# Pinning ScalarE's copy of the memory probabilities, and what follows it, in a hybrid decoder step

## The chip, the cores and the metric

The kernel runs on one core of one Trainium2 chip. The metric is device time in microseconds (us). Engines are named as the profile names them: PE is TensorE (PEld its weight loads), DVE is VectorE, ACT is ScalarE, POOL is GpSimd and SP is SyncE, which here issues most DMAs.

## The reference

One inference step of a single decoder layer, for a prompt of 4096 tokens and for 64 sample tokens (8 sequences of 8), width 1024:

```python
h = _rmsnorm(x, g_pre)
z = h @ w_in
cb, cc, ch, cg, q, k, v, ag, mq, mg = _split_cols(z)
u = cc * ch
conv = conv_w[0] * up[:, 0:t] + conv_w[1] * up[:, 1:t + 1] + conv_w[2] * up[:, 2:t + 2]
out_a = jax.nn.silu(cg) * cb * conv
out_b = jax.nn.silu(ag) * o_b      # sliding-window attention, window 128, with sinks
out_c = jax.nn.silu(mg) * o_c      # cross-attention into 256 memory tokens
y = jnp.concatenate([out_a, out_b, out_c], axis=-1) @ w_out
return x + _rmsnorm(y, g_post), new_conv, new_k, new_v
```

Window attention has 8 query heads and 2 key heads of 64; memory attention has 4 heads of 64. The sample tokens attend to cached keys and values instead of the prompt's.

## The kernel before

For more than the first half of the span the kernel projects the input (`x @ w_in`) and leaves queries, keys, values and gates in device memory. The last part, which the change touches, does attention and the output projection together, interleaved on PE.

**Attention** goes in chunks of 256 tokens (`Chunk`, 16 of them) and in halves of 128 tokens, numbered h = 2 x chunk + half. Each half has three pieces of code that are called between matmuls of the output projection. `first_half(h)` first turns the memory probabilities of the half before (`memory_transposes`, L1360 on: eight transposes on PE into the tile `tx`, then one ScalarE copy to `xp`, L1367), then issues the window scores of this half (`window_scores`, L1331), then the products of probabilities and values of the half before (`products`, L1380 on, matmuls L1388, L1394 and L1059), and then the window probabilities (ScalarE copies L1340, Vector masked copies L1341, maxima, exponentials L1287, shares L1295). `memory_half(h)` has the memory scores (L1353), their maxima, exponentials (L1178) and GpSimd's scaling (L1190). `second_half(h)` turns the window probabilities (`window_turns`, L1376), copies them on ScalarE (L1305) and masks them twice on GpSimd (L1310, L1313).

PSUM is held by three pools: `w` with two tiles of two banks, `x` with one tile of two banks, and `z` with two tiles of one bank. `tx` and the products' banks are both the one `x` tile, and so are the memory scores.

**The output projection** takes two blocks of 128 tokens (`Block`). Chunks 0 to 2 are done as plain blocks of 16 steps. Chunks 3 to 15 are done as pairs (`Pair.run`, L1721 on) with seven products in place of eight for part of the matrix, 30 steps each; a step is three matmuls (L1737), since operands are split into a rounded part and a rest (`lows`: a ScalarE cast, L1676, and a Vector subtraction, L1679). The products of a pair accumulate in four quarters of the result: c12 (block 0, right half), c21 (block 1, left), c11 (block 0, left) and c22 (block 1, right), which share the two `z` tiles in turn. Each quarter is copied or added out of its bank (`done`, L1744; `added`, L1753), squared on ScalarE for the norm (L1740), multiplied by the gain (L1749 or L1756), and at last the factor is computed (L1652 on Vector, L1653 on GpSimd) and the residual added and stored (`finish`, L1658 and L1661). The last pair's c22 is done in two pieces of 256 columns, with the whole sample between (`sample`, L1981 on), and the 64 sample tokens' own block (`Block(32)`) ends there.

Inside a pair, with its first step at e, `first_half` of the odd half is called at step e + 12, of the even half at e + 24; `memory_half` at + 16 and + 27; `second_half` at + 18 and + 32, which is step 2 of the next pair. `plain_parts` of the next pair is called at e + 20, `row_sums` at e + 27, `window_parts` at e + 4 and e + 7, `diagonal_sum` at e + 9 and `column_differences` at e + 11.

**Order.** PE's order is that of the program up to pair 12, and again from step 18 of pair 15 (`tc.manual_schedule`). All else is ordered by a planner, which takes instructions by their place in the program when their operands are there by its own model of time. `tc.keep_in_program_order(x)` adds one edge: x is issued behind the instruction of its engine that the program named just before it. It orders; it does not wait, and it keeps nothing else from standing in between. The engines other than PE work their queues in the order so made, waits included.

The sample's attention is cut into stages (generators `sample_mem(0)`, `sample_mem(1)`, `sample_window()`), and the table `steps` says at which (pair, step) each next stage is called. The scratch tiles `s3`, `s4` and `sum` have one buffer each.

## Time and profile before

| What | Value |
|---|---|
| Runs, median of 3 (lowest, highest) | 1544.68 us (1540.74, 1551.7) |
| Profiled execution, whole | 1541.58 us |
| Its span | 1539.9 us |
| PE busy | 1502.5 us, 98% |
| PEld busy | 1383.1 us, 90% |
| DVE busy | 1203.5 us, 78% |
| ACT busy | 842.8 us, 55% |
| POOL busy | 395.3 us, 26% |

The busy times are of the profiled execution, whose span is the time between its first and last instruction. A line L1367 is a line of the kernel before. In rows of a timeline the first number is the start in us from the span's beginning and the second the duration; instructions of one line are merged, and the bracket gives the idle time of the engine before the row and what released it. The ends of matmuls are modelled by the profiler. A tile's buffer numbers are left out.

### The profile page before, as it was taken

Reading aid. Unit: us, or ns where it says so; the run is one execution under the profiler, and the core shown is the slowest. Engines: PE = TensorE matmul, PEld = TensorE weight load, DVE = VectorE, ACT = ScalarE, POOL = GpSimd, SP = SyncE. Lnnn points to the kernel's source line nnn. Section 1 sums busy time; section 2 is a strip of 40 time slices with the busy share of each in tenths; the row PEclk is TensorE's granted clock in tenths of the full one; section 3 lists DMA queues with packets and bytes.
Section 4 is the critical chain, followed back from the end, with each engine's and each line's share of the span. In section 5 each row is a group of like instructions: output and inputs, shape, how many; then the busy total and the mean of one; then the engine's idle time right before and its main releaser. Section 6 shows DMA issues by size and latency. Waiting matters only on the chain. (4 is left out here: it accounts for less than half of the span.)

```text
span 1539.9 us, 30911 instructions
## 1 busy us (share of the span) xinstructions
PE 1502.5 (98%) x11497; PEld 1383.1 (90%) x11497; DVE 1203.5 (78%) x2088; ACT 842.8 (55%) x2066; POOL 395.3 (26%) x576
## 2 busy tenths in 40 slices
PE   9999999999999999999999999999999999999997
PEld 9999999999999999999999998878777777777775
DVE  6779878899888777996777688777777777777864
ACT  6776566575222222454445456666666666666652
POOL 0223322221300000000201302344444444444531
PEclk9999999999999999999999999999999999999999
DMA  9989999877755333777876978998555555555543
GB/s 262 206 209 260 262 271 270 283 245 272 193 180 180 126 126 126 255 248 272 244 252 201 252 267 248 285 260 192 166 164 165 162 160 156 155 159 156 155 149 109
DMA packets 217241, 319.70 MB, mean 208 GB/s; under 512 B 37381, under 2 KB 143365, under 8 KB 217061
## 3 DMA queue, kind: packets, MB, share of 16 engines
q1 hardware_dynamic: 196757, 273.54, 59.7%
q0 software_dynamic: 19616, 43.15, 10.2%
q8 instruction: 91, 1.49, 0.4%
q10 hardware_dynamic: 720, 1.05, 0.2%
q14 instruction: 57, 0.47, 0.1%
HBM read 208.50 MB, written 110.15 MB: 207 GB/s over the span
## 5 line engine op out<-in xcount | busy, mean ns | idle before, releaser
L375 DVE TENSOR_TENSOR z<-c,z 128x520 f32<-128x520 f32 (+1 forms) x308 | 195.0, 646 | 85.3 <-PE c L368 84.0
L1737 PE MATMUL y_c<-wo,pw 128*128 128x512 f32 (+1 forms) x636 | 159.2, 391 | 1.3 <-DVE pw L1679 0.7
L1737 PEld LDWEIGHTS y_c<-wo,pw 128*128 128x128 f32 x636 | 114.6, 188 | 27.4 <-issue 2.2
L1287 ACT ACTIVATE sm<-sm,wnm 128x128 f32<-128x128 f32 x256 | 99.4, 389 | 70.5 <-DVE wnm L1281 70.5
L1190 POOL TENSOR_SCALAR xp<-xp,xrd 128x256 f32<-128x256 f32 x128 | 67.3, 545 | 141.7 <-DVE xrd L1184 141.7
L1178 ACT ACTIVATE xp<-xs,xnm 128x256 f32<-128x256 f32 x128 | 58.8, 470 | 23.2 <-DVE xnm L1170 23.2
L1341 DVE COPY_PREDICATED sm<-wmask,ws 128x512 f32<-128x512 uint8 x60 | 40.5, 728 | 36.8 <-ACT sm L1340 36.8
L737 POOL CAST wmask<-negs 128x256 uint8<-128x256 f32 x1 | 1.0, 1049 | 263.4 <-DMA negs<-in_wmask 263.4
L1313 POOL TENSOR_SCALAR_AFFINE_SELECT wpt<-wpt 128x512 f32<-128x512 f32 x64 | 57.3, 915 | 38.5 <-ACT wpt L1305 38.1
L1637 PE MATMUL y<-wo,mh 128*128 128x512 f32 x192 | 64.6, 399 | 0.2 <-ACT y L1646 0.2
L1331 PE MATMUL ws<-kst,q 128*128 128x256 f32 (+1 forms) x480 | 55.7, 297 | 0.0
L276 ACT ACTIVATE nat<-nat 104x1024 f32<-104x1024 f32 x40 | 42.3, 1057 | 20.2 <-DMA nat<-in_x_p 20.2
L407 ACT CAST zh<-z 128x520 fp32r<-128x520 f32 x56 | 33.3, 625 | 34.8 <-DVE z L375 31.9
L377 ACT COPY z<-c 128x520 f32<-128x520 f32 (+1 forms) x44 | 24.3, 553 | 50.7 <-PE c L368 47.5
L1331 PEld LDWEIGHTS ws<-kst,q 128*128 128x128 f32 (+1 forms) x480 | 46.4, 187 | 4.1
L1658 DVE SCALAR_TENSOR_TENSOR xr<-yn,yst,xr 128x1024 f32<-128x1024 f32 (+2 forms) x34 | 46.6, 1376 | 3.0 <-POOL yst L1653 3.0
L1287 ACT ACTIVATION_READ_ACCUMULATOR sm<-sm,wnm 128x1 f32 x256 | 47.8, 187 | 0.0
L1310 POOL TENSOR_SCALAR_AFFINE_SELECT wpv<-wpt 128x512 f32<-128x512 f32 x62 | 45.5, 754 | 8.7 <-ACT wpt L1305 8.6
L1740 ACT ACTIVATE s<-yn 128x512 f32<-128x512 f32 (+1 forms) x53 | 33.4, 631 | 26.0 <-DVE yn L1753 22.4
L1295 DVE TENSOR_TENSOR sm<-sm,wrd 128x512 f32<-128x512 f32 x64 | 45.0, 703 | 1.1
L1637 PEld LDWEIGHTS y<-wo,mh 128*128 128x128 f32 x192 | 36.1, 188 | 8.9 <-issue 1.0
L164 POOL DMA_DIRECT2D md<-th x48 | 26.2, 547 | 68.1 <-DVE th L425 58.6
(1034 smaller groups left out, 5568.1 us busy)
## 6 DMA issues: line engine op xcount, KB each, us to landing
q<-qd SPq DMA_DIRECT2D x168, 128.0 KB
xr<-in_x_p SPq DMA_DIRECT2D x32, 512.0 KB
nat<-in_x_p SPq DMA_DIRECT2D x39, 416.0 KB
o_yp<-xr SPq DMA_DIRECT2D x31, 512.0 KB
kst<-qd SPq DMA_DIRECT2D x112, 128.0 KB
md<-th POOLq DMA_DIRECT2D x48, 260.0 KB
qd<-zh SPq DMA_DIRECT2D x48, 260.0 KB
qd<-z SPq DMA_DIRECT2D x48, 260.0 KB
```

Of the source, the lines that this page charges most:

```text
L276: S.activation(t[:RG], t[:RG], AF.Square, accum_out=r[:RG, i : i + 1])
L375: add = lambda dst, other: V.tensor_tensor(dst, c, other, op=ALU.add)
L1178: S.activation(p[:, i, :], s[:, i, :], AF.Exp, bias=nm[:, i : i + 1], scale=SCALE, accum_out=den[:, i : i + 1])
L1190: G.tensor_scalar(p[:, i, :], p[:, i, :], self.rds[h][:, i : i + 1], 0.5, op0=ALU.mult, op1=ALU.mult)
L1287: S.activation(sm[:, hh, :], sm[:, hh, :], AF.Exp, bias=nm[:, hh : hh + 1], scale=SCALE, accum_out=den[:, hh : hh + 1])
L1295: V.tensor_tensor(sm, sm, rd.unsqueeze(2).to_broadcast([P, 4, P]), op=ALU.mult)
L1310: G.affine_select(pv.rearrange("p (h q) -> p h q", h=4), p3, pattern=[[0, 4], [-1, P]], compare_op=ALU.is_gt, fill=0.0, base=0, channel_mu ...
L1313: G.affine_select(p3, p3, pattern=[[0, 4], [1, P]], compare_op=ALU.is_ge, fill=0.0, base=0, channel_multiplier=-1)
L1331: TE.matmul(out(kvh, col, bank), q(kvh, col, bank)[r], k(kvh, part)[r], start=first, stop=True, skip_group_check=not first, **place)
L1637: TE.matmul(acc, self.hl[l][:, k], wo[k][p][:, r], start=k + i == 0, stop=k + i == KT + 1)
L1658: x = V.scalar_tensor_tensor(self.xr[:m, cs], yn[:m, cs], st[:m, 3:4], self.xr[:m, cs], op0=ALU.mult, op1=ALU.add)
L1737: TE.matmul(acc, a[:, l, k], w[:, r, cs], start=first, stop=k == len(ws) - 1 and i == 2, skip_group_check=not new)
```

## The change

Five things change.

1. In `memory_transposes` the copy L1367 is pinned behind the ScalarE instruction named before it.
2. In a pair, `column_differences` still issues its GpSimd subtraction at its step, but the cast and the rest (`lows`, now pinned) are put in a list `between`, which `first_half` empties behind the window scores and before the products. In the last pair they come at once.
3. The Squares of a pair are pinned. `added` is cut in two: the addition stays, and `scaled` (Square, factor, gain) comes behind it; for the quarter c11 it goes into `between` also, with the block's end.
4. The intermediate of c22 is kept in `s3` until the end of the pair and no longer in `y[1]`, whose right half holds the raw differences; the sample's scratch tile moves from `s3` to `sum`.
5. The steps at which the sample's stages are called are moved, and the sample's residual is added in two halves of the columns between the pieces of the last quarter, where it was added in one, ahead of them in the program. One entry that finished a block at the first step of a pair is now only there for pair 14, at its step 27.

```diff
-            S.copy(self.xp.rearrange("p j a n -> p j (a n)"), tx)
+            tc.keep_in_program_order(S.copy(self.xp.rearrange("p j a n -> p j (a n)"), tx))
...
-                    junk = sums["s3"].tile([P, 512], F32, tag="s3", name=f"junk_s{p}")
+                    junk = sums["sum"].tile([P, 512], F32, tag="sum", name=f"junk_s{p}")
...
-        def finish(self, yn, st, dst, queued, last=False):
-            m = self.m
-            for cs in (slice(0, 512), slice(512, D)) if last else (slice(0, D),):
+        def finish(self, yn, st, dst, queued, last=False, part=None):
+            m, halves = self.m, (slice(0, 512), slice(512, D))
+            for cs in halves if last else (slice(0, D),) if part is None else (halves[part],):
...
-            self.lows(t, raw)
+            return lambda pinned=False: self.lows(t, raw, pinned)
...
-            self.sums_of(self.y[1][:, 512:], t, (self.mix(slice(0, 4), 1), self.mix(slice(0, 4), 0), ALU.subtract))
+            self.differences = self.sums_of(self.y[1][:, 512:], t, (self.mix(slice(0, 4), 1), self.mix(slice(0, 4), 0), ALU.subtract))
...
-                square(n, p, y[n][:, cs], s4)
+                square(n, p, y[n][:, cs], s4, True)
...
-            def added(n, p, acc, s, junk, cs=None):
-                cs = cs or (left_, right_)[p]
-                V.tensor_tensor(y[n][:, cs], acc, s, op=ALU.add)
-                square(n, p, y[n][:, cs], junk)
+            def added(n, p, acc):
+                cs = (left_, right_)[p]
+                V.tensor_tensor(y[n][:, cs], acc, s3 if n else y[n][:, cs], op=ALU.add)
+
+            def scaled(n, p, pinned=False):
+                cs = (left_, right_)[p]
+                square(n, p, y[n][:, cs], s4, pinned)
                 self.blocks[n].factor(st[n])
                 (V if n else G).tensor_tensor(y[n][:, cs], y[n][:, cs], gpost[:, cs], op=ALU.mult)
...
-            V.tensor_tensor(y[1][:, right_], s3, c11, op=ALU.add)
+            V.tensor_tensor(s3, s3, c11, op=ALU.add)
...
-            added(0, 0, c11, y[0][:, left_], s4)
-            ends(0)
+            added(0, 0, c11)
             if not last:
                 c22 = psum("z", f"y{c}_c22")
+                between.append(lambda: (scaled(0, 0, True), ends(0)))
                 product(c22, self.down[0], t["T6"], True)
                 product(c22, self.w[1], plain(1, range(4, 8)), False)
-                added(1, 1, c22, y[1][:, right_], s4)
+                added(1, 1, c22)
+                scaled(1, 1)
                 ends(1)
                 return
+            scaled(0, 0)
+            ends(0)
             finish_block()
-            sample()
+            rest = sample()
...
-                x = V.tensor_tensor(y[1][:, half], c22, y[1][:, half], op=ALU.add)
+                x = V.tensor_tensor(y[1][:, half], c22, s3[:, cs], op=ALU.add)
                 if p:
-                    tc.keep_in_program_order(x)
+                    rest(True, 0)
...
+            rest(True, 1)
             ends(1)
...
             chunks[c].window_scores(i)
+        while between:
+            between.pop(0)()
         banks = before[0].products(before[1]) if before else None
...
-        at(e, lambda: left.pop(0)(True) if len(left) > 1 else None)
+        if c == NCH - 2:
+            at(e + 27, lambda: left.pop(0)(True))
...
+        at(e + (9 if c == NCH - 1 else 11), lambda p=p: p.differences(True) if p.c == NCH - 1 else between.append(lambda: p.differences(True)))
...
-    steps = (((14, 16), (15, 3), (15, 6), (15, 8), (15, 10)), ((15, 8), (15, 14), (15, 16), (15, 18), (15, 21)),
-             ((14, 13), (14, 24), (15, 4), (15, 8)))
-    at(start_of(NCH - 2) + 27, lambda: left.pop(0)(True))
+    steps = (((14, 16), (14, 28), (15, 4), (15, 6), (15, 8)), ((15, 8), (15, 13), (15, 15), (15, 17), (15, 20)),
+             ((14, 13), (15, 6), (15, 15), (15, 18)))
...
-            finish_block(True)
+            return left.pop()
```

More of the change, by code (lines that the diff above doesn't have):

```diff
@@ L1647, in run @@
             self.factor(st)
-            left.append(lambda queued: self.finish(yn, st, dst, queued))
+            left.append(lambda queued, part=None: self.finish(yn, st, dst, queued, part=part))
         def factor(self, st, p=1):
@@ L1699, in row_sums @@
             raw = sums["sum"].tile([P, 512], F32, tag="sum", name=f"sum{self.c}")
-            self.sums_of(raw, t, *((self.mix(slice(2, 4), n), self.mix(slice(0, 2), n), ALU.add) for n in range(2)))
+            self.sums_of(raw, t, *((self.mix(slice(2, 4), n), self.mix(slice(0, 2), n), ALU.add) for n in range(2)))()
         def window_parts(self, n):
@@ L1707, in diagonal_sum @@
             self.diagonal = self.parts("pd")[:, :, 0:2]
-            self.sums_of(sums["sum"].tile([P, 512], F32, tag="sum", name=f"diag{self.c}"), self.diagonal, (self.mix(slice(2, 4), 0), self.mix(slice(0, 2), 1), ALU.add))
+            self.sums_of(sums["sum"].tile([P, 512], F32, tag="sum", name=f"diag{self.c}"), self.diagonal, (self.mix(slice(2, 4), 0), self.mix(slice(0, 2), 1), ALU.add))()
         def column_differences(self):
@@ L1737, in product, with square @@
                         TE.matmul(acc, a[:, l, k], w[:, r, cs], start=first, stop=k == len(ws) - 1 and i == 2, skip_group_check=not new)
-            def square(n, p, src, junk):
-                S.activation(junk, src, AF.Square, scale=float(D) ** -0.5, accum_out=st[n][:, p : p + 1])
+            def square(n, p, src, junk, pinned=False):
+                x = S.activation(junk, src, AF.Square, scale=float(D) ** -0.5, accum_out=st[n][:, p : p + 1])
+                if pinned:
+                    tc.keep_in_program_order(x)
             def done(n, p, acc):
@@ L1915, in hybrid_layer @@
     what, pending = {}, []
+    between = []
     def at(n, fn):
```

## The prediction

> **What bounds the kernel now.** I read the page first, then the waits of TensorE (PE), then busy time pair by pair, then the timeline of one pair on the four engines, and last the end of the span.
>
> ```profile
> span 1539.9 us, 30911 instructions
> ```
>
> The profiled execution took 1541.58 us, so 1.7 us lie around this span. The waits of PE (total us, times, longest) over the whole span have one large entry:
>
> ```profile
> PE wo L1388 <- ACT xp L1367: 19.6, 13, 1.7
> ```
>
> The attention products wait for ScalarE's copy of the turned memory probabilities. Busy time in one pair of the third part (length of the stretch, then PE, PEld, DVE, ACT, POOL):
>
> ```profile
> 1160.90:1198.30 37.40, 35.67 (x240) 29.10 (x239) 29.32 (x66) 23.95 (x82) 17.84 (x24) 1.00 0.58 159
> ```
>
> PE idles 1.73 us of this pair's 37.4 us and no other engine comes near to being full, so this is a TensorE kernel with one hole per pair. The timeline shows the hole in the odd half (start, duration, engine, line; idle before in brackets):
>
> ```profile
> 1159.87 2.90 PE L1737 MATMUL y_c<-wo,pw 128*128 128x512 f32 x12
> 1162.60 1.04 PE L1366 MATMUL xt<-ident,xp 128*128 128x128 f32 x8
> 1163.39 1.86 PE L1331 MATMUL ws<-kst,q 128*128 128x256 f32 x16
> 1166.88 0.43 PE L1388 MATMUL wo<-wpv,vt 64*64 64x256 f32 x2 [1.63 <-ACT xp L1367]
> ```
>
> ```profile
> 1163.97 0.62 ACT L1676 CAST pc<-yn 128x512 fp32r<-128x512 f32 x1 [4.54 <-POOL yn L1693]
> 1164.50 0.58 ACT L1744 COPY yn<-y_c 128x512 f32<-128x512 f32 x1
> 1165.11 0.63 ACT L1740 ACTIVATE s<-yn 128x512 f32<-128x512 f32 x1
> 1165.65 0.19 ACT L1740 ACTIVATION_READ_ACCUMULATOR s<-yn 128x1 f32 x1
> 1165.74 0.99 ACT L1367 COPY xp<-xt 128x1024 f32<-128x1024 f32 x1
> 1166.63 1.07 ACT L1340 COPY sm<-ws 128x512 f32<-128x512 f32 x2
> ```
>
> Transposes and products share the single two-bank tile x, so the products need the copy finished. The transposes end at 1162.60 + 1.04 = 1163.64; the copy starts only at 1165.74, behind the rounding of the differences (which stood idle 4.54 us for GpSimd, and holds ACT's queue meanwhile), the quarter's copy and its Square. The even half has the same order without the hole:
>
> ```profile
> 1179.55 1.03 PE L1366 MATMUL xt<-ident,xp 128*128 128x128 f32 x8
> 1180.34 1.86 PE L1331 MATMUL ws<-kst,q 128*128 128x256 f32 x16
> 1182.30 0.43 PE L1388 MATMUL wo<-wpv,vt 64*64 64x256 f32 x2
> ```
>
> ```profile
> 1180.53 0.63 ACT L1740 ACTIVATE s<-yn 128x512 f32<-128x512 f32 x1 [1.67 <-DVE yn L1753]
> 1181.07 0.19 ACT L1740 ACTIVATION_READ_ACCUMULATOR s<-yn 128x1 f32 x1
> 1181.16 0.99 ACT L1367 COPY xp<-xt 128x1024 f32<-128x1024 f32 x1
> 1182.06 1.07 ACT L1340 COPY sm<-ws 128x512 f32<-128x512 f32 x2
> ```
>
> The scores end at 1182.20, the products start at 1182.30: 0.1 lost.
>
> **The copy, odd half.** It is now pinned behind the last ScalarE instruction traced before it, the quarter's copy L1744. That needs only the c12 group, which ends at 1159.87 + 2.90 = 1162.77, so with its 0.58 it is over at 1163.4. The pinned copy then starts when the transposes end, about 1163.68, and ends at 1164.67, 0.58 us ahead of the end of the scores (1163.39 + 1.86 = 1165.25). The whole 1.63 goes.
>
> Not all 13 waits are of this kind. Two others:
>
> ```profile
> 1034.68 0.43 PE L1388 MATMUL wo<-wpv,vt 64*64 64x256 f32 x2 [1.66 <-ACT xp L1367]
> ```
>
> ```profile
> 1055.98 0.43 PE L1388 MATMUL wo<-wpv,vt 64*64 64x256 f32 x2 [0.25 <-ACT xp L1367]
> ```
>
> The first is half 8, at step 89, the second step of the right half of plain block 5. What was traced before it on ScalarE is the Square of that block's left half (L1646), which the change does not move, so the pin puts the copy behind just that: 1.66 stays. The second is pair 3 and goes. Left are 11 waits in pairs 4 to 14, 17.7 us. Gain: 19.6 - 1.66 = 17.9 us.
>
> **What is late next in the odd half.** The rounding starts one copy later (0.89, from 1165.74 to 1166.63): 1164.57; the window scores' copies start 0.53 after that, 1165.10, which is 0.15 ahead of the products where it was 0.25 ahead. On Vector, the low part of the differences now stands ahead of the masked copy:
>
> ```profile
> 1165.87 0.69 DVE L1749 TENSOR_TENSOR yn<-yn,gpost 128x512 f32<-128x512 f32 x1 [0.55 <-ACT s L1740]
> 1167.25 1.35 DVE L1341 COPY_PREDICATED sm<-wmask,ws 128x512 f32<-128x512 uint8 x2 [0.69 <-ACT sm L1340]
> ```
>
> The masked copy began 0.37 after the products; with the rounding over at 1165.19 and a subtraction of about 0.65 behind it (estimated as the gain multiply L1749, same shape) it begins at 1165.85, 0.6 after them. So the window softmax comes 0.2 us later relative to PE. Its last consumer:
>
> ```profile
> 1173.97 0.69 DVE L1295 TENSOR_TENSOR sm<-sm,wrd 128x512 f32<-128x512 f32 x1
> ```
>
> ```profile
> 1174.55 1.03 PE L1376 MATMUL wt<-ident,sm 128*128 128x128 f32 x8
> ```
>
> The second four transposes, at about 1174.95, need this result, there at 1174.66: 0.29 of cover, 0.2 used. Cost 0; if the cover is gone, 0.1 to 0.4 per pair.
>
> **The Squares.** Square (0,1) is traced behind the window exponentials and pinned there; its gain multiply (L1749, 0.69) leaves 1165.87 and lands between the window shares and the maxima of the memory scores, or after them; the planner decides. In the first case the memory exponentials shift by some 0.65 (its 0.69, less a little overlap). They feed GpSimd's chain into the even half's products:
>
> ```profile
> 1177.36 1.84 POOL L1190 TENSOR_SCALAR xp<-xp,xrd 128x256 f32<-128x256 f32 x4 [5.46 <-DVE xrd L1184]
> 1179.16 1.22 POOL L1310 TENSOR_SCALAR_AFFINE_SELECT wpv<-wpt 128x512 f32<-128x512 f32 x2
> 1180.33 1.22 POOL L1313 TENSOR_SCALAR_AFFINE_SELECT wpt<-wpt 128x512 f32<-128x512 f32 x2
> ```
>
> The selects end at 1181.55, with products possible at 1182.20: cover 0.65, eaten by that shift. Besides, Square (1,0) now runs behind the turned windows' copies, so its multiply, also 0.69, falls beside these selects. What that costs GpSimd, the next odd half shows:
>
> ```profile
> 1195.44 1.61 POOL L1310 TENSOR_SCALAR_AFFINE_SELECT wpv<-wpt 128x512 f32<-128x512 f32 x2
> 1197.00 2.65 POOL L1313 TENSOR_SCALAR_AFFINE_SELECT wpt<-wpt 128x512 f32<-128x512 f32 x2
> ```
>
> ```profile
> 1196.48 1.64 DVE L1658 SCALAR_TENSOR_TENSOR xr<-yn,yst,xr 128x1024 f32<-128x1024 f32 x1
> ```
>
> Beside Vector work the same selects took 0.39 and 1.43 us longer a pair. One multiply should cost the 0.39 end. So the even half loses between -0.1 (the present 0.1 goes) and 0.65 + 0.39 - 0.65 = 0.39, or 1.43 if the multiply costs the other end. I take 0.15, halfway between the first two, as it depends on the planner's order: 11 x 0.15 = 1.7 us given back.
>
> The Trainium skill ("GPSIMD Engine Reference", section 1, Specifications) says that GpSimd's SBUF interfaces are shared with VectorE and contended by Vector instructions with two SBUF inputs. The longer selects agree. By that rule, with every such overlap counted, the give-back would be the 0.39 end, 11 x 0.39 = 4.3, and the sum 2.6 us higher.
>
> Even half, rest: the copy is pinned behind the next pair's plain-part casts (traced at step 20, run long before), so it goes from 1180.6 to 1181.6; the Square follows and the scores' copies start 0.1 later. Cost 0. The s3 tile, now read to the pair's end, is a rival below. The sample's scratch tile costs nothing; its instructions are the same.
>
> **The end.** From the sample's steps to PE's last matmul, and the last stores:
>
> ```profile
> 1484.00:1530.30 46.30, 44.14 (x276) 32.78 (x274) 27.37 (x66) 17.49 (x48) 10.22 (x19) 1.00 0.37 131
> ```
>
> ```profile
> 1532.28 1.42 DVE L1658 SCALAR_TENSOR_TENSOR xr<-yn,yst,xr 128x512 f32<-128x512 f32 x2 [0.45 <-POOL yst L1653]
> ```
>
> ```profile
> 1534.91 0.52 SPq L1661 DMA_DIRECT2D o_ys<-xr  x1
> ```
>
> PE idles 2.2 us here. Moving the sample's window scores from step 24 of pair 14 to step 6 of pair 15 (with its load on SP, its small matmuls, and the copies, masks and exponentials behind them), its transposes to step 15 and its values and three stores to step 18 takes Vector work off the new pair's start and puts it beside later products. Bounds: all 2.2 gained, or as much lost; I take 1.0 gained. The stores are queued behind the sample's own load on SP, and ahead of nothing but the final stores some steps later.
>
> At the very end Vector updates block 31's two halves (to 1533.70) and then the sample, whose store goes out last at 1534.91. Now the sample's halves go first, in Vector's gaps before 1532.28, and block 31 ends about 0.1 later, so the last store leaves near 1533.8: 1.1 gained. SP issues one store more.
>
> **Sum.** 17.9 - 1.7 + 1.0 + 1.1 = 18.3 us; 1541.6 - 18.3 = 1523.3. The three runs shown lie from 1540.74 to 1551.7, median 1544.68, so the profiled one is a low one; I say 1523.5.
>
> **Rivals.** (a) GpSimd becomes the even half's last. The planner puts the multiply ahead of the maxima, and the second multiply costs up to 1.4: about 0.9 per pair, halfway between 0.39 and 1.43, 11 x 0.9 = 9.9 instead of 1.7: 1531.5. For: a cover of 0.65 against a shift of as much. Against: Vector's instruction there is short.
>
> (b) The pin does not do what it says. It orders the copy behind one instruction; it keeps nothing else from being put in between, and a late predecessor makes it late, as at 1034.68. Then only the end gains: 1539.5. Against: ScalarE had nothing ready but the rounding, now behind it.
>
> (c) Slower: the s3 tile. It has one buffer. The last quarter's addition (L1753) now reads it, and the next pair's copy of c12 (L1765) has to wait for that, while c12's next matmuls wait for the copy:
>
> ```profile
> 1191.88 0.67 DVE L1753 TENSOR_TENSOR yn<-y_c,yn 128x512 f32<-128x512 f32 x1
> ```
>
> ```profile
> 1192.54 0.60 ACT L1765 COPY s<-y_c 128x512 f32<-128x512 f32 x1
> ```
>
> ```profile
> 1194.10 2.92 PE L1737 MATMUL y_c<-wo,pr 128*128 128x512 f32 x12
> ```
>
> Today the addition ends at 1192.55 just as the copy starts, and the copy ends 0.96 before PE wants the bank. An addition later by more than 0.9 stalls PE in 12 pairs. If it slips by 3.7 us behind the maxima and shares that share Vector with it, PE loses 2.8 x 12 = 34 us, and the time is 1541.6 - 18.3 + 34 = 1557. For: the addition is not pinned and already runs late. Against: nothing that the change moves stands directly ahead of it.
>
> **How the numbers follow.** Forecast 0.58, with its own range 1518 to 1527 (bounds of the even half and the end); (a) 0.25; (b) 0.08; (c) 0.09. About 1%, 15.4 us, is what a measurement of this kernel can tell from no change. Of the forecast 0.54 lies beyond that and 0.04 within; (a) and (b) are within. So faster 0.54, same 0.37, slower 0.09. The range goes from 1517 to 1535, which takes in the forecast and (a).
>
> **What would show it.** In the new waits of PE, L1388 behind ACT L1367 should show about 1.7 us in one or two waits, not 19.6 in 13, and a pair should last about 35.9 us, not 37.4. In the odd half ScalarE should read L1744, L1367, L1676, L1340. Rival (a) would show L1388 or L1366 waiting for POOL L1313 or L1190 eleven times; (b) another ScalarE instruction between L1744 and L1367; (c) PE L1737 on pr waiting for ACT L1765. I am wrong if the pair's length does not shrink, or if the waits go and the pair still has a hole.

## The result, and the profile after

| | Kernel before | Changed kernel |
|---|---|---|
| Median of 12 runs each (lowest, highest) | 1547.09 us (1540.74, 1552.42) | 1530.89 us (1527.32, 1541.16) |
| Profiled execution, whole (its span) | 1541.58 us (1539.9) | 1541.16 us (1539.4) |

The ratio is 0.9902, with a 95% interval of 0.9879 to 0.9925: 1% faster, 15.2 us of 1547.09 (11.6 to 18.7; the two medians differ by 16.2), where 18.3 were forecast. The time itself, forecast at 1523.5, lies 7.4 us higher; 5.5 of that is the base, as the sum was made on an execution of 1541.6 us and the kernel before has a median of 1547.09 over twelve runs.

The two profiled executions are almost equally long, so they can't be compared by their spans: the changed kernel's happens to be the longest of its twelve. Windows show where it was lost. Each row gives the length of a stretch, then busy time of PE, PEld, DVE, ACT and POOL with their numbers of instructions, the granted clock of TensorE, the DMA share and GB/s. The cut is the first turning of memory probabilities. The kernel before:

```profile
0.00:818.34 818.34, 815.36 (x6777) 810.20 (x6778) 665.27 (x930) 410.66 (x694) 121.64 (x188) 1.00 0.75 224
818.34:1539.90 721.56, 687.18 (x4723) 572.93 (x4721) 538.21 (x1159) 432.10 (x1372) 273.67 (x389) 0.99 0.65 189
```

The changed kernel:

```profile
0.00:831.47 831.47, 823.12 (x6777) 816.48 (x6778) 666.19 (x930) 410.19 (x694) 118.79 (x188) 1.00 0.75 221
831.47:1539.40 707.93, 687.67 (x4723) 570.28 (x4721) 541.92 (x1160) 432.95 (x1372) 272.69 (x389) 0.99 0.68 192
```

The input projection, which the change doesn't touch, took 13.1 us more in this one execution; among the profiles of this study it takes 818 to 832 us. From the cut to the end the changed kernel is 13.6 us shorter at the same busy time of PE: what went is idle time. All that follows is read behind the cut.

The waits of PE over the span (total us, times, longest), the changed kernel:

```profile
PE y_c L1737 <- DVE yn L1755: 3.8, 11, 0.6
PE wt L1376 <- DVE sm L1295: 2.1, 11, 0.4
...
PE wo L1388 <- ACT xp L1367: 1.7, 1, 1.7
```

The row that stood at 19.6 us in 13 waits is down to the one at half 8. In its place stand two rows, 5.9 us together, of which the first wasn't there and the second stood at 0.3 us in one wait. One pair, from the transposes of an even half to those of the next (the kernel before measured between odd halves):

```profile
1162.60:1199.57 36.97, 35.24 (x237) 28.75 (x236) 28.89 (x65) 23.95 (x82) 17.41 (x24) 1.00 0.59 161
```

```profile
1155.11:1190.90 35.79, 35.31 (x237) 28.59 (x236) 29.26 (x65) 24.02 (x82) 17.14 (x24) 1.00 0.60 166
```

A pair is 1.18 us shorter, with 0.48 us of idle time left in it, where it had 1.73. The odd half, changed kernel, PE and ScalarE (start, duration, engine, line; idle before in brackets):

```profile
1175.32 1.03 PE L1366 MATMUL xt<-ident,xp 128*128 128x128 f32 x8
1176.11 1.85 PE L1331 MATMUL ws<-kst,q 128*128 128x256 f32 x16
1177.89 0.43 PE L1388 MATMUL wo<-wpv,vt 64*64 64x256 f32 x2
```

```profile
1175.52 0.59 ACT L1746 COPY yn<-y_c 128x512 f32<-128x512 f32 x1 [3.34 <-PE y_c L1737]
1176.44 1.01 ACT L1367 COPY xp<-xt 128x1024 f32<-128x1024 f32 x1 [0.34 <-PE xt L1366]
1177.36 0.62 ACT L1676 CAST pc<-yn 128x512 fp32r<-128x512 f32 x1
1177.88 1.07 ACT L1340 COPY sm<-ws 128x512 f32<-128x512 f32 x2
```

ScalarE's order is the predicted one (L1744 has become L1746): the copy L1367 waits for the transposes and for nothing else, and the products follow the scores without a hole. The window scores' copies now start with the products; they started 0.25 us ahead of them before. Where the two new waits arise, on VectorE and PE:

```profile
1167.62 0.67 DVE L1755 TENSOR_TENSOR yn<-y_c,s 128x512 f32<-128x512 f32 x1
```

```profile
1167.64 0.38 PE L1912 MATMUL vtp<-ident,vT 128*128 128x128 f32 x2
1168.35 1.65 PE L1737 MATMUL y_c<-wtT,pa 128*128 128x512 f32 x6 [0.33 <-DVE yn L1755]
```

```profile
1184.93 0.66 DVE L1169 TENSOR_REDUCE xmx<-xs 128x2 f32<-128x512 f32 x1
1185.51 0.68 DVE L1295 TENSOR_TENSOR sm<-sm,wrd 128x512 f32<-128x512 f32 x1
```

```profile
1185.58 0.60 PE L1376 MATMUL wt<-ident,sm 128*128 128x128 f32 x4
1186.34 0.63 PE L1376 MATMUL wt<-ident,sm 128*128 128x128 f32 x4 [0.16 <-DVE sm L1295]
```

First, the second product of the next pair (T4) needs the bank of the old pair's last quarter, which is free when VectorE has done that quarter's addition (L1755, L1753 before). Second, the last four transposes of the odd half's window probabilities need the second share (L1295), which stands behind a maximum of the memory scores.

### The profile page after: what moved, and what is told of

Its sections match the earlier page's. It is cut to its first block, busy times and chain, and to the rows that moved or that the text cites. A ratio compares the mean times of both kernels' runs of the same rounds, so it can differ in the third digit from the quotient of the medians.

```text
span 1539.4 us, 30947 instructions
## 1 busy us (share of the span) xinstructions
PE 1510.8 (98%) x11497; PEld 1386.8 (90%) x11497; DVE 1208.1 (78%) x2089; ACT 843.1 (55%) x2066; POOL 391.5 (25%) x576
## 4 chain that ended last, share of the span: by engine, by line
PE 68%; DVE 12%; issue 4%; DMA 4%; ACT 3%; POOL 1%; SPq 1%; DVEq 0%; ACTq 0%; POOLq 0%
PE c L368 49%; PE y_c L1737 9%; PE y L1637 2%; DVE sm L1295 2%; DVE sm L1341 1%; PE xt L1366 1%; DVE xr L1658 1%; DMA kst<-qd 1%; PE ws L1331 1%; DVE xmx L1169 1%; ACT sm L1287 1%; DMA nat<-in_x_p 1%; DVE wmx L1279 1%; PE mem_acc L790 1%; DMA zs<-in_w_out 1%
## 5 line engine op out<-in xcount | busy, mean ns | idle before, releaser
L1737 PE MATMUL y_c<-wo,pw 128*128 128x512 f32 (+1 forms) x636 | 158.4, 391 | 0.5 <-DVE yn L1775 0.5
L1737 PEld LDWEIGHTS y_c<-wo,pw 128*128 128x128 f32 x636 | 114.1, 188 | 27.2 <-issue 5.4
L1310 POOL TENSOR_SCALAR_AFFINE_SELECT wpv<-wpt 128x512 f32<-128x512 f32 x62 | 51.8, 848 | 58.5 <-ACT wpt L1305 58.4
L1658 DVE SCALAR_TENSOR_TENSOR xr<-yn,yst,xr 128x1024 f32<-128x1024 f32 (+2 forms) x35 | 52.4, 1501 | 3.1 <-POOL yst L1653 3.0
L1295 DVE TENSOR_TENSOR sm<-sm,wrd 128x512 f32<-128x512 f32 x64 | 44.8, 700 | 1.1
L1367 ACT COPY xp<-xt 128x1024 f32<-128x1024 f32 x30 | 30.4, 1014 | 27.1 <-POOL wpv L1310 16.1
L1737 PE MATMUL y_c<-wtT,pa 128*128 128x512 f32 x156 | 41.1, 400 | 3.8 <-DVE yn L1755 3.8
```

The source lines that it names most:

```text
L1295: V.tensor_tensor(sm, sm, rd.unsqueeze(2).to_broadcast([P, 4, P]), op=ALU.mult)
L1658: x = V.scalar_tensor_tensor(self.xr[:m, cs], yn[:m, cs], st[:m, 3:4], self.xr[:m, cs], op0=ALU.mult, op1=ALU.add)
L1737: TE.matmul(acc, a[:, l, k], w[:, r, cs], start=first, stop=k == len(ws) - 1 and i == 2, skip_group_check=not new)
```

## The experiments

Nine kernels were run, each beside runs of the kernel before on the same chip, which took 1546.93 us there for e1 to e4, 1549.3 for e5 to e7 and 1545.88 for e8 and e9 (medians). So the ratios are what is comparable; the length of a pair, read in each profile, is much sharper than any total. Edits shift the lines: L1737, L1746, L1755 and L1775 of the changed kernel have higher numbers in some rows below, and the text says what they are.

| Kernel | Median us (runs) | Ratio to before, 95% | A pair, us |
|---|---|---|---|
| changed kernel | 1530.89 (12) | 0.990 (0.988 to 0.992) | 35.79 |
| e1, differences only | 1540.2 (7) | 0.995 (0.993 to 0.998) | 36.52 |
| e2, Squares only | 1535.18 (4) | 0.992 (0.989 to 0.994) | 36.52 |
| e3, old end | 1529.14 (4) | 0.987 (0.985 to 0.990) | 35.80 |
| e4, addition first | 1529.9 (4) | 0.988 (0.985 to 0.990) | 35.79 |
| e5, no hole at half 8 | 1529.94 (4) | 0.988 (0.986 to 0.989) | 35.80 |
| e6, quarter chain | 1531.21 (6) | 0.989 (0.987 to 0.991) | 35.90 |
| e7, e6 with e3 and e5 | 1533.85 (5) | 0.990 (0.988 to 0.992) | 35.90 |
| e8, early cast | 1526.39 (6) | 0.987 (0.984 to 0.989) | 35.63 |
| e9, e8 with e5 | 1528.75 (6) | 0.988 (0.985 to 0.991) | 35.63 |

**e1: the Squares go back**, unpinned and right behind the additions; only the rounding of the differences is moved.

```diff
-                square(n, p, y[n][:, cs], s4, True)
+                square(n, p, y[n][:, cs], s4)
...
             added(0, 0, c11)
+            scaled(0, 0)
+            ends(0)
...
-                between.append(lambda: (scaled(0, 0, True), ends(0)))
```

> The changed kernel with the Squares (and what follows them) put back where they were; only the rounding of the differences is moved. ScalarE's order in the odd half is then quarter's copy, Square, xp copy, rounding. Theory (the rounding, which waits for GpSimd, is what held the copy): the copy ends 0.15 us ahead of the scores, the eleven waits of 1.6 us stay away, and a pair lasts 35.6 to 36.0 us (35.8 in the changed kernel, 37.0 before), since TensorE's new wait for the last quarter's addition (L1755, 0.33 a pair) shrinks and the one for the window shares (L1295, 0.16) grows. Rival (the Square also has to go): its 0.63 us stays in front, about 0.5 us of wait per odd half remains, and a pair lasts 36.3 or more.

A pair took 36.52 us, and the hole was in neither place. The waits of PE in e1:

```profile
PE wt L1376 <- DVE sm L1295: 11.5, 13, 1.1
PE y L1632 <- DVE mh_s L1605: 2.1, 1, 2.1
PE wo L1388 <- ACT xp L1367: 1.6, 1, 1.6
```

Its odd half, ScalarE, then VectorE, then PE:

```profile
1164.56 0.63 ACT L1740 ACTIVATE s<-yn 128x512 f32<-128x512 f32 x1
...
1165.19 0.99 ACT L1367 COPY xp<-xt 128x1024 f32<-128x1024 f32 x1
1166.09 0.61 ACT L1676 CAST pc<-yn 128x512 fp32r<-128x512 f32 x1
1166.61 1.07 ACT L1340 COPY sm<-ws 128x512 f32<-128x512 f32 x2
```

```profile
1173.35 0.68 DVE L1169 TENSOR_REDUCE xmx<-xs 128x2 f32<-128x512 f32 x1
...
1174.02 0.68 DVE L1169 TENSOR_REDUCE xmx<-xs 128x2 f32<-128x512 f32 x1
...
1174.82 0.69 DVE L1295 TENSOR_TENSOR sm<-sm,wrd 128x512 f32<-128x512 f32 x1
```

```profile
1175.65 0.63 PE L1376 MATMUL wt<-ident,sm 128*128 128x128 f32 x4 [1.06 <-DVE sm L1295]
```

The Square ahead of the copy makes the scores' copies 0.28 us late against the products, which start at 1166.33 without a wait, and the planner now puts both maxima (2 x 0.68) ahead of the second share. So L1388's wait goes by moving the rounding alone, and what moving the Squares buys is the place where the time would come back. The totals of e1 hold another loss, behind the last pair (the 2.1 us row). The new wait behind L1755 isn't in e1's list: the quarter c11's Square stands in its old place there, and the even half runs as before the change.

**e2: the differences go back**, rounded at their own step, unpinned; only the Squares are moved.

```diff
-        at(e + (9 if c == NCH - 1 else 11), lambda p=p: p.differences(True) if p.c == NCH - 1 else between.append(lambda: p.differences(True)))
+        at(e + (9 if c == NCH - 1 else 11), lambda p=p: p.differences(p.c == NCH - 1))
```

> The changed kernel with the rounding of the differences given at its step again; only the Squares are moved. ScalarE's order in the odd half is rounding, quarter's copy, xp copy. Theory: the rounding still waits for GpSimd, the copy starts 1.45 us late, and L1388 waits 1.0 us for L1367 in each odd half; a pair lasts 36.8 us, and some 11 of the changed kernel's gain are lost. Rival (the Squares were in the way): the waits stay away and a pair lasts 35.8.

The wait of PE in e2:

```profile
PE wo L1388 <- ACT xp L1367: 12.4, 12, 1.7
```

Without half 8 that is 10.7 us in 11 waits: ten of 0.9 us, near the theory's 1.0, and one of 1.64. A pair took 36.52 us (36.8 expected). So with the Square alone out of the way the hole shrinks by 0.7 us; what is left is the rounding, which holds the queue while it waits for GpSimd. With the rounding alone out of the way (e1) the hole closes, but the softmax behind it comes late. For the pair's length both had to leave. The wait behind L1755 is in e2's list, at 3.5 us in 11 waits, so it comes with the moved Squares.

**e3: the old end**, that is the sample's steps and the order of the last stores as before the change.

```diff
-    steps = (((14, 16), (14, 28), (15, 4), (15, 6), (15, 8)), ((15, 8), (15, 13), (15, 15), (15, 17), (15, 20)),
-             ((14, 13), (15, 6), (15, 15), (15, 18)))
+    steps = (((14, 16), (15, 3), (15, 6), (15, 8), (15, 10)), ((15, 8), (15, 14), (15, 16), (15, 18), (15, 21)),
+             ((14, 13), (14, 24), (15, 4), (15, 8)))
...
-            return left.pop()
+            finish_block(True)
```

> The changed kernel with the sample's steps and the sample's last addition as they were before. Theory (the new end is worth nothing, as the two profiles show): pairs last 35.8 us, and from the last even half to the last matmul, and from there to the end, it takes 51.5 and 9.6 us, within 0.5 of the changed kernel's 51.9 and 9.6. Rival (the prediction's terms): 1.0 and 1.1 us longer.

Nothing was lost by it; the stretch came out shorter than the changed kernel's by more than the 0.5 us that the theory allowed. From the last transposes of memory probabilities to PE's last matmul it took 51.12 us (51.86 in the changed kernel, 51.51 before), and from there to the end of the span 9.41 (9.58 and 9.63). The new end cost 0.7 and 0.2 us: six other profiles that have it (e2, e4, e5, e6, e8 and e9) show 51.70 to 51.83 and 9.57 to 9.58, so two profiles of one end differ by less. It is one profile of the old end behind these pairs, and behind those of e6 the old end took longer (e7, below).

**e4: the addition first.** On VectorE the next pair's row-sum subtraction is pinned behind the last quarter's addition instead of standing ahead of it.

```diff
-            self.sums_of(raw, t, *((self.mix(slice(2, 4), n), self.mix(slice(0, 2), n), ALU.add) for n in range(2)))()
...
+            S.copy(t[:, 0], raw)
+            behind.append(lambda: self.low(t, raw))
...
                 added(1, 1, c22)
+                while behind:
+                    behind.pop(0)()
```

> The changed kernel with Vector's subtraction for the next pair's row sums put behind the last quarter's addition, which today waits behind it. Theory (TensorE's new wait of 0.33 us a pair is Vector's queue in front of that addition, which frees the bank): the wait for L1755 goes, nothing else takes its place, and a pair lasts 35.45 us, 12 pairs 4 us less than the changed kernel. Rival (something else is late by as much): the wait moves to the rows' product, behind the subtraction, and a pair stays at 35.8.

The wait went from the list and the pair stayed at 35.79: the rival's length, for neither of the reasons given. To see where the time had gone, the starts of the same PE instructions were laid side by side, as offsets from the start of the pair's even transposes (medians over the eleven or twelve pairs of one profile; the kernel before in the first column):

| Start of, us into the pair | before | changed | e4 | e6 | e8 |
|---|---|---|---|---|---|
| T4 product | 13.06 | 13.22 | 12.64 | 12.65 | 12.65 |
| row-sum products | 14.55 | 14.71 | 14.41 | 14.12 | 14.12 |
| first window-mixture product | 17.30 | 17.43 | 17.34 | 17.33 | 16.88 |
| odd half's transposes (L1366) | 20.05 | 20.19 | 20.15 | 20.16 | 19.63 |
| odd half's turned windows (L1376) | 31.97 | 30.45 | 30.41 | 30.43 | 29.90 |
| the product behind them | 32.76 | 31.59 | 31.60 | 31.71 | 31.43 |
| next even transposes | 36.97 | 35.79 | 35.80 | 35.91 | 35.64 |

The changed kernel is 1.52 us ahead of the kernel before at the odd half's turned windows and 1.17 at the product behind them: 0.35 are lost at the second share, where the list of waits shows 0.19 a pair, as it counts only idle time behind the modelled ends of matmuls.

In e4 the T4 product starts 0.58 us earlier than in the changed kernel, the row sums only 0.30, the mixture 0.09. So the addition was one link, with others right behind it. At the turned windows (L1376) its list of waits has 2.8 us, 1.9 of it under another name, where the changed kernel has 2.1.

**e6: the quarter chain.** On top of e4, the last quarter's Square goes behind the copy of the next pair's first product, and its multiply behind the next pair's first subtraction.

```diff
-                scaled(1, 1)
...
+                    later.append(lambda: (square(1, 1, y[1][:, right_], s4, True), self.blocks[1].factor(st[1])))
+                    later.append(lambda: V.tensor_tensor(y[1][:, right_], y[1][:, right_], gpost[:, right_], op=ALU.mult))
...
-            S.copy(s3, c12)
+            tc.keep_in_program_order(S.copy(s3, c12))
+            if later:
+                later.pop(0)()
```

> The kernel of e4 (the last quarter's addition ahead of the row sums' subtraction on VectorE), and the last quarter's Square goes behind the copy of the next pair's first product, its multiply behind the next pair's first subtraction. In e4 the T4 product started 0.57 us earlier in the pair, but the row-sum products won only 0.30, the products behind them 0.10 and the pair nothing. Theory: that 0.57 was given back in two queues, 0.27 on ScalarE (the copy L1765 stood behind the Square L1740) and 0.20 on VectorE (the addition L1772 behind the multiply L1761); with both out of the way a pair lasts 35.25 us, not 35.79, and the time falls by 10 x 0.54 = 5.4 us against the changed kernel. Rival: VectorE is full in this stretch whatever its order, and the wait goes to the shares of the window probabilities (wt behind L1295) or to the parts of the mixture: a pair lasts 35.6 to 35.8.

Half of the theory held: the row sums now start the full 0.59 us earlier, so the copy had indeed stood behind the Square. But the next product wins 0.10 only, and a pair takes 35.90 us, more than the rival said: the turned windows start where they did, and the product behind them 0.12 us later. VectorE, ScalarE and PE there:

```profile
1158.08 0.69 DVE L1679 TENSOR_TENSOR pw<-place,pw 128x512 fp32r<-128x512 f32 x1 [0.67 <-ACT pw L1676]
1158.69 0.68 DVE L1787 TENSOR_TENSOR yn<-s,y_c 128x512 f32<-128x512 f32 x1
```

```profile
1156.44 1.09 ACT L1305 COPY wpt<-wt 128x512 f32<-128x512 f32 x2
1157.38 0.66 ACT L1676 CAST pw<-place 128x512 fp32r<-128x512 f32 x1
```

```profile
1159.52 3.01 PE L1747 MATMUL y_c<-wo,pw 128*128 128x512 f32 x12 [0.30 <-DVE yn L1787]
```

VectorE isn't full, as the rival had it: it stands idle for 0.67 us, for a cast that waits in ScalarE's queue behind the copies of the turned windows. What one queue lets go, the next one keeps.

**e8: the early cast.** On top of e6, that cast is taken where ScalarE waits for the maxima anyway.

```diff
             S.copy(t[:, 0], raw)
+            if self.c < NCH - 1:
+                w = self.w[0] = self.parts("pw0_")
+                S.copy(w[:, 0], self.mix(slice(4, 8), 0))
...
```

> e6 with one ScalarE cast moved: the upper part of the next pair's first window mixture (pw, L1676) is taken right behind the cast of the row sums, where ScalarE waits 1.56 us for the maxima, and no longer behind the copies of the turned window probabilities; VectorE's subtraction for the diagonal sum is kept behind the pair's second difference, so that it doesn't come in between. In e6 the T4 product and the row sums started 0.57 to 0.59 us earlier and the product behind them only 0.11, because VectorE waited 0.67 us for that cast (at 1158.08), and PE 0.30 behind VectorE. Theory (ScalarE's queue behind the exponentials was the last keeper of that time): the wait of PE behind the first subtraction goes, a pair lasts 35.35 us (0.57 less than the changed kernel's 35.79, 0.12 more for the shares that e6 delayed), and the time falls by 11 x 0.45 = 5 us against the changed kernel. Rival (the pair is bound by the softmax round from one half to the next, whatever the order within it): 35.7 or more, with the wait at the transposes behind L1295 grown by as much.

Now the whole 0.56 us is carried through half a pair, to the turned windows at 29.90. There 0.39 of it is lost, and a pair takes 35.63 us: between theory and rival, nearer to the rival. PE's wait in e8:

```profile
1172.11 0.60 PE L1376 MATMUL wt<-ident,sm 128*128 128x128 f32 x4
1173.31 0.63 PE L1376 MATMUL wt<-ident,sm 128*128 128x128 f32 x4 [0.60 <-ACT yn L1764]
```

The view names a copy of ScalarE that these transposes don't read, and which ended at 1173.27. VectorE's second share, which they do read, ended 0.11 us earlier:

```profile
1172.48 0.68 DVE L1295 TENSOR_TENSOR sm<-sm,wrd 128x512 f32<-128x512 f32 x1
```

It stands behind a maximum as in the changed kernel, and PE went on 0.15 us after it; in the changed kernel the share ended at 1185.51 + 0.68 = 1186.19 and PE followed 0.15 later, in e1 at 1175.51 and 0.14. PE's weight load for these transposes starts 0.12 us behind the share's end in all three (1173.28, 1186.31, 1175.62), while the copy ended 0.01 ahead of the load in e8, 0.06 after it in the changed kernel and 0.84 ahead of it in e1. So it is the share, and with it the softmax round that the odd half's transposes start, as the rival had it. Moving the share ahead of the maxima was not tried. What speaks against it is that GpSimd's scaling ends at 1176.10 + 1.83 = 1177.93 in e8, just when the next even transposes start, at 1177.91:

```profile
1176.10 1.83 POOL L1190 TENSOR_SCALAR xp<-xp,xrd 128x256 f32<-128x256 f32 x4
```

**e5: no hole at half 8.** One Square, that of block 5's left half, goes behind the window scores' copies.

```diff
-                S.activation(acc[:m], acc[:m], AF.Square, scale=float(D) ** -0.5, accum_out=st[:m, p : p + 1])
+                square = lambda acc=acc, p=p: S.activation(acc[:m], acc[:m], AF.Square, scale=float(D) ** -0.5, accum_out=st[:m, p : p + 1])
+                if (b, p) == (5, 0):
+                    held.append(square)
+                else:
+                    square()
...
+            while held:
+                tc.keep_in_program_order(held.pop()())
             dens = [self.window_exps(b, kvh, sm) for kvh, sm in enumerate(self.sms)]
```

> The changed kernel with one ScalarE instruction moved: the Square of the left half of block 5 (L1646) goes behind the two copies of window scores of half 8 instead of ahead of the copy of that half's probabilities (L1367). It is the only hole of the old kind that is left: L1388 waits 1.67 us behind L1367 at 1047.84, and the matmuls behind it showed a granted clock of 0.86 to 0.88 and took 24.4 us from half 8's transposes to the next ones where the kernel before took 22.7. Theory (the lower clock comes from the hole): L1388's wait goes, the clock stays near its neighbours' and the stretch from half 8's transposes to the next ones lasts 21.0 us, 1.7 under the 22.7 with the hole and 3.4 under the 24.4 with hole and drop; the time falls by 1.7 to 3.4 us against the changed kernel. Rival (the clock's drop comes by chance or from the kind of work, not from the hole): the stretch lasts 22.7 with a clock of 0.86 to 0.88 in it although nothing waits there.

The changed kernel, then e5, from half 8's transposes to the next ones:

```profile
1043.52:1067.90 24.38, 22.26 (x132) 17.45 (x131) 16.79 (x35) 12.42 (x42) 12.03 (x16) 0.93 0.90 255
```

```profile
1036.87:1058.35 21.48, 21.03 (x133) 16.80 (x132) 16.55 (x35) 12.44 (x42) 12.06 (x16) 1.00 0.96 284
```

The hole went and the clock is whole. Of 1.67 us 1.2 were kept (21.48 against the 22.72 of the kernel before, with the hole and a whole clock); the rest of the 2.9 is the clock. With the hole the clock fell here in 2 of 8 profiles (the changed kernel's and e2's), without it in none of 3 (e5, e7, e9); more on this in the last section. In the totals the 1.7 to 3.4 us can't be told: the intervals of e5 and the changed kernel overlap.

**e7 and e9: together.** e7 is e6 with the edits of e3 and e5; e9 is e8 with that of e5.

> e6 with the moved Square of e5, and the sample's steps and the last stores as they were before the change (e3, which was 0.7 us faster at the end of the kernel than the changed kernel). Theory: the three do not meet, as they lie at half 8, in the pairs and behind the last pair; so 1.7 to 3.4, 5.4 and 0.7 add up to 8 to 9.5 us less than the changed kernel, about 1521 us. Rival: as in e6, 3 us less at most.

> e8 with the Square of block 5 moved as in e5. Theory: the two don't meet; a pair of 35.35 us, no hole at half 8, and from the eighth group of transposes to the last one 465.7 - 5 = 460.7 us, where the changed kernel's profile had 468.6 and e5's 465.7; the time is 6 to 8 us below the changed kernel's. Rival: as in e8, 1.3 us below.

e7 took 1533.85 us, where 1521 were expected. e6's gain, the largest part, isn't there, and the old end doesn't suit e6 (52.34 us from the last transposes to PE's last matmul, 51.79 in e6). Behind the cut e7's profile has 706.7 us, 1.0 less than e6's; the input projection alone took 828.6 us in it. In e9 the parts do add up in the profile: 702.9 us behind the cut, the shortest of all (e8 704.1, the changed kernel 707.9), from the eighth group of transposes to the last 463.5 us against the 460.7 expected. Its median, 1528.75, is not below e8's, and the 6 to 8 us expected against the changed kernel aren't shown by the totals. Against the kernel before, e8's ratio and the changed kernel's, taken on different chips, overlap by a little, and by its pairs e8 wins 11 x 0.16 = 1.8 us. It is the best candidate that was found; that it beats the changed kernel is likely and not shown.

## Why the prediction was right, and where it was off

The direction, the hole and its removal, and the range held; what takes time back and what the end is worth did not. The forecast was 3 us too high in gain. Its terms against what the profiles show:

| Term | Predicted | Measured |
|---|---|---|
| L1388's waits removed | 17.9 | 17.9 (19.6 to 1.7) |
| given back | 1.7 | 5.9 (3.8 and 2.1) |
| sample's new steps | +1.0 | -0.35 (51.51 to 51.86) |
| last store | +1.1 | +0.05 (9.63 to 9.58) |
| sum | 18.3 | 11.7 |
| clock behind the holes, not in the sum | none | +1.6 |

That makes 13.3 of the 13.6 us that the profiles differ by behind the cut. (By starts, the second of the new waits costs more than the list says, 0.35 us a pair, and the even half's products start 0.17 us earlier than before; in the sum the two nearly cancel.)

The medians differ by more, 16.2 us, and the clock is a likely reason. Both profiled executions have a mean granted clock of 0.996. The 32 runs of the kernel before that stood beside the experiments have a median of 0.995 (0.992 to 0.997), the twelve of the changed kernel 0.998 (0.996 to 0.998). A share of 0.003 of 1547 us is 4.6 us, an estimate, and 3 to 6 with the rounding of these figures. With it in place of the 1.6, the terms make 16.3 us. So that the forecast of 18.3 came out near is luck in part: its own terms were worth 11.7, and a term that it didn't have filled much of the gap.

- *The copy, odd half, and the exception at half 8*: right. One wait of 1.7 us is left, at the place named.
- *Even half, rest: "the scores' copies start 0.1 later. Cost 0."* This is the step that failed. The copies did start later, 0.15 us relative to the transposes: 2.51 us behind them before (1182.06 and 1179.55), 2.66 after, by these rows of PE and ScalarE:

```profile
1155.13 1.04 PE L1366 MATMUL xt<-ident,xp 128*128 128x128 f32 x8
```

```profile
1157.79 1.07 ACT L1340 COPY sm<-ws 128x512 f32<-128x512 f32 x2
```

The whole softmax came later with them, and at its end so did the quarter's addition (it ends 13.00 us behind the transposes before, 13.16 after), while PE came to that place 0.16 us earlier. Together that is the 0.33 us of wait, since there was no margin: in all eleven pairs of both profiles T4 starts 0.05 to 0.06 us behind the addition's end. The trace of before had shown it. The addition ended at 1192.55, as quoted for rival (c); T4 began right then, and its weight load already waited for the addition, though PE had no idle time in front of T4:

```profile
1192.60 1.66 PE L1737 MATMUL y_c<-wtT,pa 128*128 128x512 f32 x6
```

```profile
1192.60 0.53 PEld L1737 LDWEIGHTS y_c<-wtT,pa 128*128 128x128 f32 x3 [0.23 <-DVE yn L1753]
```

The addition's row was read for the copy behind it and not for the bank that the addition frees. The price was about 0.33 us in each of eleven pairs (0.59 in one, which lasts 36.4 us). e1 and e2 confirm the cause: with the Squares in their old places the addition ends at 13.00 us and T4 waits 0.02 us at most (0.10 in the last pair); with them moved it ends at 13.16, and all eleven wait. VectorE's finish (L1658), which took 1.83 us in place of 1.28 on the way, isn't the cause: with the instruction behind it, it took 1.91 and 1.90 (last section).
- *Odd half: "0.29 of cover, 0.2 used. Cost 0"*: 0.5 were used, 0.36 by the masked copies (at 1178.62, 0.73 us behind the products and not 0.6; 0.37 before) and the rest by a maximum (0.66 us) that the planner now puts ahead of the second share, where a subtraction of 0.40 stood. The bound given for a lost cover, 0.1 to 0.4, holds the 0.19 of the list and the 0.35 by starts.
- *GpSimd's selects, 0.15 a pair*: the even half did end 0.14 us later, for another reason (T4, above), so the size is luck. The first copy of the turned windows (1187.00) now goes ahead of the memory exponentials, so GpSimd does its first two selects early, and it isn't late. Rival (a) fell with that.
- *Rival (b)*, the pin does nothing, was refuted in its result and is right in its letter: the kernel before with that one pin added keeps its order on all engines, and so does the changed kernel without it. What works is moving the rounding and the Squares in the program, by e1 and e2 (with pins of their own, which weren't tried apart; the Square of c22 has none, though the list of changes speaks of all). The prediction credited the copy's pin.
- *Rival (c)*, the s3 tile: no wait of T4's successors behind the copy in the changed kernel; but e4 and e6 showed that this copy stands next in line.
- *The end*: predicted as 2.1 us gained, it cost 0.3 between the two profiles and 0.9 against e3. The idle time of the sample's part was no reserve that other steps could reach, and the last store, sent 0.9 us earlier relative to PE's last matmul (3.8 us behind it where it was 4.7), did not bring the end of the span nearer. What the span's last microseconds wait for, the trace doesn't show.
- *The pair's length of 37.4 us* was that of the window quoted, which began ahead of the transposes; from transposes to transposes it was 36.97. Against that the predicted 1.5 us were 1.18, and the 35.9 us came near to the measured 35.79 because both ends of the difference were off. Of its signs of being wrong, one came true in small: the old waits went, and the pair still has 0.48 us of idle time.

## What to carry to other kernels

When a wait is removed, list every resource that the released engine asks for in the next loop round, with the margin of each, before costing any at nothing: here a place without margin, at which PE showed no idle time but its weight load a wait of 0.23 us, took back 0.33 us per round. Fixing such a wait alone may move nothing, since the next queue keeps the time; lay the starts of the same instructions side by side in both traces, and the place where the offset is lost again names the next keeper. And ask of an ordering edge whether it changes the order at all, since the moved code may do the work.

## What the runs showed of the hardware

**The clock behind a hole.** The granted clock of TensorE fell behind some of the holes of about 1.6 us. The kernel before, one of two such pairs (the other, 1366.10 to 1404.74, has 38.64 us at the same clock), and the stretch of that pair at which the clock was 0.50:

```profile
1253.50:1292.13 38.63, 36.91 (x238) 29.81 (x236) 29.35 (x64) 24.16 (x82) 17.40 (x24) 0.96 0.57 154
1278.41:1281.82 3.41, 3.41 (x27) 2.49 (x24) 2.52 (x7) 1.27 (x7) 0.00 (x0) 0.50 1.08 346
```

Each pair took 1.66 us more than its neighbours, at a clock of 0.96, and nothing waited longer in it. The half clock began 0.6 us behind the end of the pair's hole (1277.79) and lasted 3.41 us, half of which is 1.7. Behind the cut, the changed kernel has one such stretch (from 1047.98, 3.41 us at 0.50), behind its only such hole:

```profile
1047.84 0.60 PE L1388 MATMUL wo<-wpv,vt 64*64 64x256 f32 x2 [1.67 <-ACT xp L1367]
```

These two matmuls take 0.43 us elsewhere. Over the eleven profiles, from 20 us on to PE's last matmul, there are six such stretches. Each is 3.41 us long and begins within 2.0 us of the end of a hole of 1.6 us or more; behind 16 other holes of 1.5 us or more the clock stayed whole, and which ones it falls behind the runs don't show. The Trainium skill ("TensorE: Matmul & The Clock Gate", Part 1) has the clock halved by an activity monitor with a window of about 3.4 us; one window at half clock would cost 1.7 us by that page, as an estimate, and the 1.66 agrees. It states a whole idle window as the condition, and a hole of 1.67 us is half of that; the measurement decides that shorter holes can be enough, in some cases. So a hole can cost twice its length.

**Vector and GpSimd side by side.** The finish of a block (L1658) met GpSimd's row sum in both kernels; in the kernel before Vector's took 1.28 us and GpSimd's 1.79:

```profile
1186.36 1.28 DVE L1658 SCALAR_TENSOR_TENSOR xr<-yn,yst,xr 128x1024 f32<-128x1024 f32 x1
```

```profile
1186.45 1.79 POOL L1693 TENSOR_TENSOR sum<-mix 128x256 f32<-128x256 f32 x1 [3.14 <-DVE wes L1283]
```

In the changed kernel Vector's took 1.83 and GpSimd's 0.74:

```profile
1162.10 1.83 DVE L1658 SCALAR_TENSOR_TENSOR xr<-yn,yst,xr 128x1024 f32<-128x1024 f32 x1
```

```profile
1162.12 0.74 POOL L1693 TENSOR_TENSOR sum<-place 128x256 f32<-128x256 f32 x1 [2.36 <-DVE wes L1283]
```

They started within 0.1 us of each other in both cases, Vector first. But Vector lost as much in the kernel before, in its next instruction; the kernel before, then the changed kernel:

```profile
1187.56 0.70 DVE L1292 TENSOR_TENSOR wden<-wden,wes 128x4 f32<-128x4 f32 x1
```

```profile
1163.86 0.15 DVE L1292 TENSOR_TENSOR wden<-wden,wes 128x4 f32<-128x4 f32 x1
```

From the start of L1658 to the end of L1292 Vector took 1.90 and 1.91 us, in ten pairs of each profile alike (1.89 to 1.91); in the changed kernel's last pair, beside other work on GpSimd, it took 1.39. So GpSimd's time changed with the order of work, and Vector's, taken over both instructions, did not; the longer L1658 cost nothing by itself. The prediction had only GpSimd pay for the shared interface; here Vector paid in both kernels.
